# Mean squares of q and k: two float32r products of a split square in place of one float32 product

## The chip, the cores and the metric

The kernel runs on one core of a Trainium2 chip. The metric is device time in microseconds (us). Engines are named as in the profile: PE (matrix products and transposes), PEld (PE's weight loads, a row of its own), DVE (VectorE), ACT (ScalarE), POOL (GpSimd), SP (the queue that starts most transfers).

## What is computed

Two layers of a hybrid backbone work on 1024 latent tokens and 256 context tokens. The part that matters here is the normalisation of queries and keys, ahead of two kinds of attention (A: a window, with rotary positions; B: a neighbourhood on a grid):

```
def rms_norm(x, g):
    x32 = x.astype(jnp.float32)
    y = x32 * lax.rsqrt(jnp.mean(x32 * x32, axis=-1, keepdims=True) + EPS)
    return (y * g.astype(jnp.float32)).astype(x.dtype)
...
    qa = rope_2d(rms_norm(aq.reshape(bsz, t_len, A_HEADS, HEAD_DIM), a_qn))
    ka = rope_2d(rms_norm(ak.reshape(bsz, t_len, A_KV_HEADS, HEAD_DIM), a_kn))
...
    qb = rms_norm(bq.reshape(bsz, t_len, B_HEADS, HEAD_DIM), b_qn)
    kb = rms_norm(bk.reshape(bsz, t_len, B_HEADS, HEAD_DIM), b_kn)
```

The mean runs over the 64 channels of a head.

## The kernel before

Activations lie transposed: channels on the 128 partitions, tokens along the free dimension, in three chunks of 512, 512 and 256 tokens. Nearly all projections and attention products take float32 operands that were split into a float32r high part and a float32r rest; `split` does it with a cast on ACT and a subtraction on DVE, `split_w` for weights with a cast on ACT and a subtraction on POOL. A projection is then three products, high by high, high by rest and rest by high.

A channel block of 128 holds two heads. For each such block of q or k (a "pair"), `qk_norm` is called once for each chunk when the projection's last product is done. It squares the projection on ACT into `sq`, multiplies it with the gain on DVE into `raw`, and puts `finish` on a timer of T["ms"] ns. `finish` multiplies `sq` with a 128x128 matrix `blk` (two 64x64 blocks of 1/64) in one float32 product, which gives every channel the mean square of its head. DVE adds epsilon (`me`, L743), ACT and DVE make the inverse root in the buffer of `sq` (L749 to L754), the rotary of branch A runs on DVE and POOL (L758 to L761), and `to_dram` splits the result on POOL (L771, L772) and sends it to DRAM, from where attention loads it.

A layer has 39 such calls: in branch B four pairs with k and q, in branch A one k block and four q pairs, three chunks each. In all there are 78, of which 52 have 512 columns and 26 have 256.

PE's instructions are in program order. The other engines' order comes from a scheduler. The program order is made while the kernel is built, by the class `Weave`: a clock `W.now` goes forward by an assumed time for every product (`mm`: n / 0.6 ns for float32, n * 17 / 38.4 for float32r), `W.later` puts a piece of work on a timer of that clock, and between timed pieces the clock's owner takes "dense" work, first q, k and v projections (`need`), then gate projections (`spare`, tiles gt and sg). The attention itself is a chain of steps no closer than T["pace"] ns. Products end in PSUM tiles of the tags d, s, t and o; the mean square takes one of the three t tiles, which the transposes of the attention weights (pt) also use.

Tiles have a fixed number of buffers, here `qraw` 2 (also used for the cached keys and values, kc and vc, and for the v projection, vr) and `qsq` 2. Whoever takes a buffer waits for the last user of the tile that had it before.

Of the kernel before, what the change touches and what calls it, by code (L numbers as in the profile page):

```python
# [15 lines left out]
P = 128  # L16
# [9 lines left out]
HD = 64  # L26
# [50 lines left out]
PSB = {"d": 2, "s": 2, "t": 3, "o": 1}  # L77
LGB = ("s", "t")
LDB = ("d", "t")
T = dict(f1=9, f2=2, kc=10000, c0=10000, cq=1, gx=3, nx=8000, yo=1500, yi=1000, aq=9000, ac=7000, ms=2000, v=3200, tok=8600, scale=1100, t0=3400, tb=2200, o=2200, soft=7600, pace=9000, lg=320, lr=8500, cv=16000, le=4200)  # L80


class Weave:
# [107 lines left out]
def trunk(nc, tc, ctx, I, K, O):  # L191
# [46 lines left out]
    nc.scalar.dma_start(cst[:, :384], K["k_const"][:, :384])  # L238
    nc.scalar.dma_start(cst[:, 384:], K["k_const"][:, 768:])
    ident, blk, ones_d, sel = cst[:, 0:128], cst[:, 128:256], cst[:, 256:384], cst[:, 384:386]  # L240
    fill = cp.tile([P, 2], F32, name="fill")
    nc.vector.memset(fill[:, 0:1], EPS)
    nc.vector.memset(fill[:, 1:2], 1e-37)
# [182 lines left out]
    def split(hi, lo, x):  # L426
        nc.scalar.copy(hi, x)  # L427
        nc.vector.tensor_sub(lo, x, f32(hi))  # L428
# [40 lines left out]
    def blocked(t):  # L469
        return t.rearrange("p (r a c) -> p a r c", r=8, a=8)  # L470
# [256 lines left out]
    def attention(l, H, ap):  # L727
# [2 lines left out]


        def qk_norm(ps, N, gain, rope_c0, name, then, blocks=False):
            raw = ap.tile([P, 512], F32, tag="qraw", name=f"{name}_raw", bufs=2)
            sq = ap.tile([P, 512], F32, tag="qsq", name=f"{name}_sq", bufs=2)
            src, to = (blocked(ps), in_blocks) if blocks else (ps, lambda t: t)
            nc.scalar.activation(to(sq[:, :N]), src, AF.Square)
            nc.vector.tensor_scalar(to(raw[:, :N]), src, gain, None, ALU.mult)

            def finish():
                ms = ps_tile("t", f"{name}_ms")  # L740
                mm(ms[:, :N], blk, sq[:, :N], True, True)
                me = cp.tile([P, 512], F32, tag="g2", name=f"{name}_me", bufs=3)
                nc.vector.tensor_scalar(me[:, :N], ms[:, :N], EPS, None, ALU.add)  # L743
                if not loaded:
                    exp_ln(me[:, :N])
                    loaded.append(True)
                rs = sq

                nc.scalar.activation(rs[:, :N], me[:, :N], AF.Ln)  # L749
                nc.scalar.activation(rs[:, :N], rs[:, :N], AF.Exp, scale=-0.5)  # L750
                nc.vector.tensor_tensor(raw[:, :N], raw[:, :N], rs[:, :N], ALU.mult)
                nc.scalar.activation(rs[:, :N], rs[:, :N], AF.Square)
                nc.vector.tensor_tensor(rs[:, :N], me[:, :N], rs[:, :N], ALU.mult)
                nc.vector.scalar_tensor_tensor(raw[:, :N], rs[:, :N], -3.0, raw[:, :N], ALU.add, ALU.mult)  # L754
                if rope_c0 is not None:
                    cs = ap.tile([P, 2, 512], F32, tag="stage", name=f"{name}_cs", bufs=2)
                    dma(cs, K["k_rope"][:, :, rope_c0:rope_c0 + N])
                    nc.vector.stream_shuffle(rs, raw, [(i + 16) % 32 for i in range(32)])  # L758
                    nc.gpsimd.tensor_tensor(rs, rs, cs[:, 1], ALU.mult)
                    nc.gpsimd.tensor_tensor(raw, raw, cs[:, 0], ALU.mult)  # L760
                    nc.gpsimd.tensor_add(raw, raw, rs)  # L761
                then(raw[:, :N])
            W.later(T["ms"], finish)
# [17 lines left out]
        def k_jobs(br, p, cond):  # L781
            name = f"{br}{l}_{p}"
            perm, rope = br == 1, br == 0
            c0w = O_BK + p * P if br else O_AK
            h0 = 2 * p if br else 0
            out = O[4] if br else O[2]

            def start():
                t = ap.tile([P, 4, P], F32, tag="qraw", name=f"kc{name}", bufs=2)
                src = I["cache_kb"] if br else I["cache_ka"]  # L790
                dma(t, src[0, l, :, h0:h0 + 2].rearrange("(j p) h d -> p j (h d)", p=P))

                def cached():
                    pt = ps_tile("t", f"kct{name}")
                    for j in range(4):
                        transpose(pt[:, j * P:(j + 1) * P], t[:, j], ident)
                    to_dram(pt, NPAST, f"kc{name}", k_put(br, p, NTOK, NPAST), True)
                W.later(T["kc"], cached)

            def evac(ci, ps):  # L800
                c0, N = CHUNKS[ci]

                def then(kn):
                    if c0 >= NLAT:
                        def to_tokens():
                            pt = ps_tile("t", f"kt{name}")
                            for j in range(2):
                                transpose(pt[:, j * P:(j + 1) * P], kn[:, j * P:(j + 1) * P], ident)
                            ko = ap.tile([P, 2, P], F32, tag="Y", name=f"ko{name}", bufs=2)
                            nc.scalar.copy(ko, pt[:, :2 * P].rearrange("p (j m) -> p j m", j=2))  # L810
                            dma(out[0, l, :, h0:h0 + 2].rearrange("(j p) h d -> p j (h d)", p=P), ko)
                        W.later(T["tok"], to_tokens)
                    to_dram(kn, N, f"k{name}_{ci}", k_put(br, p, c0, N))
                    W.mark(("K", br, l, p, ci), 4000)
                qk_norm(ps, N, dcol[l][:, 2 * br + 1:2 * br + 2], c0 if rope and c0 < NLAT else None,
                        f"k{name}_{ci}", then, perm and c0 < NLAT)
            W.need.append((cond, job(w_in, c0w, (0, 1, 2), lambda ci: H.cols(ci), evac, f"k{name}", start)))

        def v_jobs(br, p, cond):
# [5 lines left out]

            def evac(ci, ps):
                c0, N = CHUNKS[ci]
                vr = ap.tile([P, 512], F32, tag="qraw", name=f"vr{name}_{ci}", bufs=2)
                lat = perm and c0 < NLAT
                nc.scalar.copy(in_blocks(vr) if lat else vr[:, :N], blocked(ps) if lat else ps)  # L830

# [45 lines left out]
        class Keys:  # L877
# [16 lines left out]

            def load_v(c):
                h0 = 2 * c.p if c.br else 0
                t = ap.tile([P, 4, 2, HD], F32, tag="qraw", name=f"vc{c.name}", bufs=2)
                src = I["cache_vb"] if c.br else I["cache_va"]
                dma(t, src[0, l, :, h0:h0 + 2].rearrange("(j p) h d -> p j h d", p=P))
                c.V = {}  # L900
                for n, b0, nb in (("lat", 0, 8), ("ctx", 8, 2)):
                    c.V[n] = ap.tile([P, nb, 2, 2, HD], F32R, tag=f"V{n}", name=f"V{n}{c.name}")
                    dma(f32(c.V[n]), v_d[l][c.br][c.p][:, b0:b0 + nb])
                c.V["past"] = ap.tile([P, 4, 2, 2, HD], F32R, tag="Vpast", name=f"Vpast{c.name}")
                split(c.V["past"][:, :, :, 0], c.V["past"][:, :, :, 1], t)
                c.at["V"] = W.now + 7000
# [631 lines left out]
```

## Time and profile before

| what | value |
|---|---|
| median of 3 runs | 3151.2 us (3148.72 to 3158.55) |
| the profiled execution's own time | 3155.3 us |
| its span, from first to last instruction | 3153.5 us |
| its mean granted TensorE clock | 0.992 |
| PE busy | 3080.7 us, 98% |
| PEld busy | 2629.2 us, 83% |
| DVE, ACT, POOL busy | 1786.2 us, 1708.8 us, 971.1 us |

The times of one engine add up over instructions. PE's matrix instructions overlap in time, so their durations do not say how often one can start; the distance of their starts does.

### The profile page before, as it was taken

How to read it: one execution, taken by the hardware profiler on the slowest of the kernel's cores; microseconds unless marked ns; L12 is line 12 of the kernel's file. 1: busy time of each engine (PE TensorE's matmuls, PEld its weight loads, DVE VectorE, ACT ScalarE, POOL GpSimd, SP SyncE). 2: the span in 40 equal slices, each digit the busy share in tenths (PEclk: the TensorE clock that was granted, in tenths of full speed). 3: DMA queues.
4: the chain of work that ended last, by engine and by line, in shares of the span. 5: the costliest groups of instructions: out<-in, count | busy, mean ns of one | idle time of the engine just before them, and what ended most of it. 6: DMA issues, size and time to landing. Idle time of an engine off the chain costs nothing.

```text
span 3153.5 us, 48110 instructions
## 1 busy us (share of the span) xinstructions
PE 3080.7 (98%) x17421; PEld 2629.2 (83%) x17421; DVE 1786.2 (57%) x3293; ACT 1708.8 (54%) x3591; POOL 971.1 (31%) x815
## 2 busy tenths in 40 slices
PE   8999999999999999999999999999999999999999
PEld 5777788888888888888888888888888888888887
DVE  5666366666666664355463553665675666655431
ACT  4677355555556564343356873655555556654422
POOL 3454322222222121245343443222231221112632
PEclk8999999999999999999999999999999999999999
DMA  8654555545532332663442226455555332347543
GB/s 277 174 177 136 162 142 152 157 110 160 157 99 81 96 94 79 225 203 115 147 146 70 79 91 183 118 147 147 138 142 154 95 96 80 98 140 241 163 146 101
DMA packets 447434, 435.03 MB, mean 138 GB/s; under 512 B 75120, under 2 KB 368604, under 8 KB 445916
## 3 DMA queue, kind: packets, MB, share of 16 engines
q1 hardware_dynamic: 441212, 414.92, 44.1%
q0 software_dynamic: 5664, 16.83, 1.6%
q8 instruction: 137, 2.24, 0.3%
q14 instruction: 101, 0.83, 0.1%
q10 hardware_dynamic: 320, 0.21, 0.0%
HBM read 298.12 MB, written 137.29 MB: 138 GB/s over the span
## 4 chain that ended last, share of the span: by engine, by line
PE 64%; DVE 6%; POOL 3%; ACT 2%; issue 2%; DMA 2%; SPq 0%; ACTq 0%; POOLq 0%; DVEq 0%
PE gt L218 14%; PE sg L218 10%; PE br L218 6%; PE o L218 5%; PE po L218 5%; PE pt L225 5%; PE q L218 4%; PE sc L218 3%; PE k L218 3%; PE v L218 2%; PE sl L218 2%; PE cx L218 2%; POOL acc L1242 1%; PE lg L218 1%; DVE gl L1241 1%
## 5 line engine op out<-in xcount | busy, mean ns | idle before, releaser
L427 ACT CAST PT<-pt 128x512 fp32r<-128x512 f32 (+2 forms) x528 | 273.3, 536 | 304.2 <-PE pt L225 299.8
L428 DVE TENSOR_TENSOR PT<-pt,PT 128x512 fp32r<-128x512 f32 (+2 forms) x528 | 320.9, 622 | 99.3 <-ACT PT L427 96.6
L981 DVE TENSOR_REDUCE st<-sc 128x1 f32<-128x512 f32 x256 | 176.0, 687 | 269.8 <-PE sc L218 269.3
L218 PE MATMUL gt<-hhl,wgt_h 128*128 128x512 f32 x736 | 299.3, 407 | 1.4 <-ACT wgt_h L422 1.3
L218 PE MATMUL gt<-hhl,wgt_l 128*128 128x512 f32 x736 | 290.2, 394 | 1.1 <-POOL wgt_l L423 1.1
L218 PE MATMUL gt<-hll,wgt_h 128*128 128x512 f32 x736 | 290.0, 394 | 0.0
L225 PE MATMUL pt<-cst,P 128*128 128x128 f32 x1856 | 272.7, 273 | 4.6 <-ACT ko L810 4.1
L423 POOL TENSOR_TENSOR wgt_l<-wgt_r,wgt_h 128x512 fp32r<-128x512 f32 x110 | 174.0, 1590 | 290.2 <-ACT wgt_h L422 280.4
L225 PEld LDWEIGHTS pt<-cst,P 128*128 128x128 f32 x1856 | 217.6, 141 | 9.7 <-ACT ko L810 4.5
L218 PE MATMUL po<-z,wpo_h 128*128 128x512 f32 (+1 forms) x768 | 211.2, 362 | 7.2 <-ACT z L427 4.5
L218 PE MATMUL br<-yl,wbr_h 128*128 128x512 f32 (+1 forms) x576 | 205.2, 356 | 1.6 <-DVE yl L428 1.6
L218 PE MATMUL br<-yh,wbr_h 128*128 128x512 f32 (+1 forms) x576 | 204.7, 355 | 0.3 <-DVE gl L1241 0.3
L218 PE MATMUL br<-yh,wbr_l 128*128 128x512 f32 (+1 forms) x576 | 204.4, 355 | 0.0
L1003 ACT ACTIVATE P<-sc,st 128x512 f32<-128x512 f32 x256 | 175.2, 684 | 53.7 <-DVE st L997 52.8
L423 POOL TENSOR_TENSOR wsg_l<-wsg_r,wsg_h 128x512 fp32r<-128x512 f32 x48 | 66.3, 1387 | 374.7 <-ACT wsg_h L422 353.3
L1005 ACT ACTIVATE P<-sl,st 128x384 f32<-128x384 f32 (+1 forms) x320 | 170.7, 533 | 17.6 <-DVE st L993 17.3
L218 PE MATMUL sc<-Kpast,Q 128*128 128x512 f32 x512 | 168.3, 410 | 9.0 <-ACT P L1003 9.0
L218 PE MATMUL o<-PT,Vpast 128*128 128x256 f32 x1024 | 176.0, 294 | 0.9 <-DVE PT L428 0.3
L218 PEld LDWEIGHTS gt<-hhl,wgt_l 128*128 128x128 f32 x736 | 138.5, 188 | 33.8 <-POOL wgt_l L423 1.5
L218 PEld LDWEIGHTS gt<-hhl,wgt_h 128*128 128x128 f32 x736 | 139.0, 189 | 32.6 <-issue 4.7
L218 PEld LDWEIGHTS po<-z,wpo_h 128*128 128x128 f32 x768 | 136.1, 190 | 31.9 <-ACT z L427 5.8
L218 PEld LDWEIGHTS gt<-hll,wgt_h 128*128 128x128 f32 x736 | 139.2, 189 | 25.8 <-issue 0.5
(350 smaller groups left out, 8535.7 us busy)
## 6 DMA issues: line engine op xcount, KB each, us to landing
Q<-q_d SPq DMA_DIRECT2D x160, 256.0 KB
gl<-g_d SPq DMA_DIRECT2D x48, 640.0 KB
wgt_r<-in_w_in_dram SPq DMA_DIRECT2D x110, 256.0 KB
g_d<-tgt SPq DMA_DIRECT2D x92, 256.0 KB
wa<-in_w_ada_dram POOLq DMA_DIRECT2D x64, 256.0 KB, 4.0
wpo_r<-in_w_out_dram SPq DMA_DIRECT2D x64, 256.0 KB
yg<-y_d SPq DMA_DIRECT2D x24, 640.0 KB
yr<-s_d SPq DMA_DIRECT2D x24, 640.0 KB
```

The costliest lines, as they stand in the source:

```text
L218: nc.tensor.matmul(out, a, b, start=start, stop=stop)
L225: nc.tensor.transpose(out, x, idn)
L423: nc.gpsimd.tensor_sub(lo, r, f32(hi))
L427: nc.scalar.copy(hi, x)
L428: nc.vector.tensor_sub(lo, x, f32(hi))
L981: nc.vector.tensor_reduce(cm, psc, AX.X, ALU.min)
L1003: nc.scalar.activation(pt[:, nl * P:(nl + 4) * P], psc, AF.Exp, bias=m, scale=-1.0, accum_out=sums[:, t, x, 1:2])
L1005: nc.scalar.activation(pt[:, :nl * P], loc, AF.Exp, bias=m, scale=-1.0, accum_out=sums[:, t, x, 0:1])
L1241: nc.vector.scalar_tensor_tensor(g, g, 1.0, ps, ALU.add, ALU.mult)
L1242: (nc.vector if b == 0 and k >= KD - 2 else nc.gpsimd).tensor_add(z, z, g)
```

## The change

The sum over a head's channels is taken from the square's two float32r parts, in two products that add up in one PSUM tile, with a float32r copy of `blk`. The parts have a tile of their own, `qtwo`, which has one buffer (the pool's default). `split` is called right behind the square and the gain, ahead of the timer. `qraw` and `qsq` get three buffers. T["ms"] goes from 2000 to 4500, T["pace"] from 9000 to 8800. The descriptor space of the transfers that POOL starts goes from its default of 16384 to 8192 bytes per partition. The four other lines that changed name qraw's new buffer count.

```
-T = dict(f1=9, f2=2, kc=10000, c0=10000, cq=1, gx=3, nx=8000, yo=1500, yi=1000, aq=9000, ac=7000, ms=2000, v=3200, tok=8600, scale=1100, t0=3400, tb=2200, o=2200, soft=7600, pace=9000, lg=320, lr=8500, cv=16000, le=4200)
+T = dict(f1=9, f2=2, kc=10000, c0=10000, cq=1, gx=3, nx=8000, yo=1500, yi=1000, aq=9000, ac=7000, ms=4500, v=3200, tok=8600, scale=1100, t0=3400, tb=2200, o=2200, soft=7600, pace=8800, lg=320, lr=8500, cv=16000, le=4200)
...
     ident, blk, ones_d, sel = cst[:, 0:128], cst[:, 128:256], cst[:, 256:384], cst[:, 384:386]
+    blk_r = cp.tile([P, P], F32R, name="blk_r")
+    nc.scalar.copy(blk_r, blk)
...
         def qk_norm(ps, N, gain, rope_c0, name, then, blocks=False):
-            raw = ap.tile([P, 512], F32, tag="qraw", name=f"{name}_raw", bufs=2)
-            sq = ap.tile([P, 512], F32, tag="qsq", name=f"{name}_sq", bufs=2)
+            raw = ap.tile([P, 512], F32, tag="qraw", name=f"{name}_raw", bufs=3)
+            sq = ap.tile([P, 512], F32, tag="qsq", name=f"{name}_sq", bufs=3)
             src, to = (blocked(ps), in_blocks) if blocks else (ps, lambda t: t)
+
             nc.scalar.activation(to(sq[:, :N]), src, AF.Square)
             nc.vector.tensor_scalar(to(raw[:, :N]), src, gain, None, ALU.mult)
+            two = ap.tile([P, 2, 512], F32R, tag="qtwo", name=f"{name}_two")
+            split(two[:, 0, :N], two[:, 1, :N], sq[:, :N])

             def finish():
                 ms = ps_tile("t", f"{name}_ms")
-                mm(ms[:, :N], blk, sq[:, :N], True, True)
+                mm(ms[:, :N], blk_r, two[:, 0, :N], True, False)
+                mm(ms[:, :N], blk_r, two[:, 1, :N], False, True)
...
-    nc = bacc.Bacc("TRN2", target_bir_lowering=False, num_devices=1)
+    nc = bacc.Bacc("TRN2", target_bir_lowering=False, num_devices=1, dynamic_dma_scratch_size=8192)
```

How PE's order changes shows at the start of the first layer's attention. The names are those of pair 0: k_0_1 and k_0_2 are its second and third chunk of k, q_0_0 the first chunk of q, k_0_1_ms and k_0_2_ms their mean squares. The projection of k_0_1 ended before these rows. Before:

```order
L218 MATMUL k_0_2_3369<-hhc_5_1040,wk_0_4_l 128x256
L218 MATMUL k_0_1_ms<-k_0_1_sq,cst 128x512
L218 MATMUL k_0_2_3369<-hhc_6_1049,wk_0_4_h 128x256
...
L218 MATMUL k_0_2_3369<-hhc_7_1058,wk_0_4_l 128x256
L218 MATMUL q_0_0_3425<-hhl_0_230,wq_0_0_h 128x512
...
L218 MATMUL q_0_0_3425<-hhl_2_234,wq_0_0_l 128x512
L218 MATMUL k_0_2_ms<-k_0_2_sq,cst 128x256
L218 MATMUL q_0_0_3425<-hhl_3_236,wq_0_0_h 128x512
```

And now:

```order
L218 MATMUL q_0_0_3422<-hll_2_237,wq_0_0_h 128x512
L218 MATMUL q_0_0_3422<-hhl_2_236,wq_0_0_l 128x512
L218 MATMUL k_0_1_ms<-k_0_1_two,blk_r 128x512 x2
L218 MATMUL q_0_0_3422<-hhl_3_238,wq_0_0_h 128x512
...
L218 MATMUL q_0_0_3422<-hhl_5_242,wq_0_4_l 128x512
L218 MATMUL k_0_2_ms<-k_0_2_two,blk_r 128x256 x2
L218 MATMUL q_0_0_3422<-hhl_6_244,wq_0_4_h 128x512
```

Both mean squares have moved back by several projection products, and the third chunk's now stands nine products of 512 columns behind the second's, where before there were fifteen (six of 256 columns and nine of 512).

On ACT the cast of the split stands between the other work. The same place, with what each row waits for in brackets (PE, DVE, Pool, Activation are engines, DMAHW and DMASW transfers). Before:

```order
L736 ACTIVATE k_0_1_sq<-k_0_1_3309 128x512 [waits DMASW4_49,DMASW3_49,DMASW6_49,DMASW2_49,DMASW7_49,DMASW0_49,PE_49]
L752 ACTIVATE k_0_0_sq<-k_0_0_sq 128x512 [waits DVE_49]
L422 CAST wv_0_0_h<-wv_0_r_3413 128x512 [waits DMAHW5_49,PE_49,Pool_49]
L427 CAST kc_0_st<-kct_0_3349 128x512 [waits DMASW6_49,DMASW2_49]
L422 CAST wv_0_4_h<-wv_0_r_3419 128x512 [waits DMAHW6_49,PE_49,Pool_49]
L749 ACTIVATE k_0_1_sq<-k_0_1_me 128x512 [waits DVE_49,Activation_49]
L736 ACTIVATE k_0_2_sq<-k_0_2_3369 128x256 [waits PE_49]
```

And now:

```order
L739 ACTIVATE k_0_1_sq<-k_0_1_3314 128x512 [waits PE_49]
L756 ACTIVATE k_0_0_sq<-k_0_0_sq 128x512 [waits Activation_49]
L429 CAST k_0_1_two<-k_0_1_sq 128x512 [waits Activation_49]
L739 ACTIVATE k_0_2_sq<-k_0_2_3378 128x256 [waits PE_49]
L424 CAST wv_0_0_h<-wv_0_r_3410 128x512 [waits DMAHW5_49,Pool_49]
L758 ACTIVATE k_0_0_sq<-k_0_0_sq 128x512 [waits DVE_49]
L424 CAST wv_0_4_h<-wv_0_r_3416 128x512 [waits DMAHW6_49,Pool_49]
L429 CAST k_0_2_two<-k_0_2_sq 128x256 [waits PE_49,Activation_49]
L429 CAST kc_0_st<-kct_0_3358 128x512 [waits DMASW6_49,DMASW2_49]
L755 ACTIVATE k_0_1_sq<-k_0_1_me 128x512 [waits DVE_49]
```

Two casts have come in. The second, k_0_2_two, waits for PE: its buffer is free only when the products of k_0_1_ms have read it.

## Rows read from the trace of the kernel before

**Rows 1.** The page's part 1: busy time, share of the span, instructions.

```profile
PE 3080.7 (98%) x17421; PEld 2629.2 (83%) x17421; DVE 1786.2 (57%) x3293; ACT 1708.8 (54%) x3591; POOL 971.1 (31%) x815
```

**Rows 2.** Both attention stages: PE, PEld, DVE, ACT, POOL busy; PEclk, DMA, GB/s.

```profile
326.00:1262.00 936.00, 917.85 (x5473) 802.13 (x5473) 567.09 (x1241) 526.86 (x1348) 224.54 (x204) 0.99 0.43 123
1890.00:2810.00 920.00, 905.39 (x5426) 785.94 (x5425) 567.36 (x1239) 522.90 (x1341) 220.35 (x200) 1.00 0.45 124
```

**Rows 3.** What PE waited for: total us, times, longest.

```profile
PE q_ms L218 <- ACT q_sq L736: 6.0, 2, 3.0
...
PE pt L225 <- ACT ko L810: 4.1, 2, 2.1
PE vt L225 <- ACT vr L830: 3.6, 2, 2.1
```

**Rows 4.** Timeline of PE around two mean squares (start, duration, instruction).

```profile
347.87 1.02 PE L218 MATMUL k_ms<-k_sq,cst 128*128 128x512 f32 x2
348.32 0.68 PE L218 MATMUL k<-hhc,wk_h 128*128 128x256 f32 x1
348.84 0.28 PE L218 MATMUL k<-hlc,wk_h 128*128 128x256 f32 x1
348.96 0.28 PE L218 MATMUL k<-hhc,wk_l 128*128 128x256 f32 x1
...
351.50 0.59 PE L218 MATMUL k_ms<-k_sq,cst 128*128 128x256 f32 x2
351.75 0.58 PE L218 MATMUL q<-hhl,wq_h 128*128 128x512 f32 x1
352.16 0.39 PE L218 MATMUL q<-hll,wq_h 128*128 128x512 f32 x1
352.39 0.40 PE L218 MATMUL q<-hhl,wq_l 128*128 128x512 f32 x1
```

**Rows 5.** Groups of the mean squares' tiles: duration ns min/median/max, first and last start, forms.

```profile
L218 PE MATMUL q_ms<-q_sq,cst x96: 377/591/796, 357.4 to 2678.1; 128*128 128x512 f32 x64, 128*128 128x256 f32 x32
...
L218 PEld LDWEIGHTS k_ms<-k_sq,cst x60: 186/189/192, 340.7 to 2333.2; 128*128 128x128 f32 x60
L218 PE MATMUL k_ms<-k_sq,cst x60: 377/592/644, 340.9 to 2333.4; 128*128 128x512 f32 x40, 128*128 128x256 f32 x20
```

**Rows 6.** ACT's cast of a 128x512 tile, by line: busy, mean ns.

```profile
L422 ACT CAST wgt_h<-wgt_r 128x512 fp32r<-128x512 f32 x110 | 66.8, 621 | 40.7 <-DMA wgt_r<-in_w_in_dram 21.5 <-PE q L218 9.2 <-PE gt L218 3.3
```

**Rows 7.** DVE on k's tiles: two SBUF sources (L751), one PSUM source (L743, q).

```profile
L751 DVE TENSOR_TENSOR k_raw<-k_raw,k_sq x30: 396/692/1720, 345.3 to 2338.1; 128x512 f32<-128x512 f32 x20, 128x256 f32<-128x256 f32 x10
...
L743 DVE TENSOR_SCALAR q_me<-q_ms x48: 404/680/693, 358.8 to 2680.4; 128x512 f32<-128x512 f32 x32, 128x256 f32<-128x256 f32 x16
```

**Rows 8.** Timeline of all engines at 902 us, idle time before in brackets.

```profile
901.89 2.98 POOL L423 TENSOR_TENSOR wgt_l<-wgt_r,wgt_h 128x512 fp32r<-128x512 f32 x2
901.95 1.79 DVE L751 TENSOR_TENSOR q_raw<-q_raw,q_sq 128x512 f32<-128x512 f32 x1
903.66 1.23 DVE L1000 TENSOR_TENSOR st<-st,sink 128x1 f32<-128x1 f32 x1
904.92 0.29 ACT L1001 ACTIVATE st<-sink,st 128x1 f32<-128x1 f32 x1 [2.15 <-DVE st L1000]
...
907.29 1.22 PE L218 MATMUL q_ms<-q_sq,cst 128*128 128x256 f32 x2 [3.04 <-ACT q_sq L736]
```

**Rows 9.** Timelines at 780 and 811 us.

```profile
780.54 0.75 DVE L737 TENSOR_SCALAR q_raw<-q,dcol 128x512 f32<-128x512 f32 x1 [1.30 <-POOL k_st L772]
...
783.02 0.44 PE L225 MATMUL pt<-cst,P 128*128 128x128 f32 x2 [2.07 <-ACT ko L810]
...
810.89 0.59 ACT L830 COPY vr<-v 128x512 f32<-128x512 f32 x1 [3.73 <-POOL q_st L772]
```

**Rows 10.** ACT's timeline at the kernel's start.

```profile
7.98 0.22 ACT L331 ACTIVATE sl<-ccol 128x16 f32<-128x16 f32 x1 [4.10 <-DVE ccol L330]
```

**Rows 11.** The page's part 3: the queue of POOL's transfers: packets, MB, share.

```profile
q0 software_dynamic: 5664, 16.83, 1.6%
```

More of the change, by code (lines that the diff above doesn't have):

```diff
@@ L788, in start @@
             def start():
-                t = ap.tile([P, 4, P], F32, tag="qraw", name=f"kc{name}", bufs=2)
+                t = ap.tile([P, 4, P], F32, tag="qraw", name=f"kc{name}", bufs=3)
                 src = I["cache_kb"] if br else I["cache_ka"]
@@ L827, in evac @@
                 c0, N = CHUNKS[ci]
-                vr = ap.tile([P, 512], F32, tag="qraw", name=f"vr{name}_{ci}", bufs=2)
+                vr = ap.tile([P, 512], F32, tag="qraw", name=f"vr{name}_{ci}", bufs=3)
                 lat = perm and c0 < NLAT
@@ L896, in load_v @@
                 h0 = 2 * c.p if c.br else 0
-                t = ap.tile([P, 4, 2, HD], F32, tag="qraw", name=f"vc{c.name}", bufs=2)
+                t = ap.tile([P, 4, 2, HD], F32, tag="qraw", name=f"vc{c.name}", bufs=3)
                 src = I["cache_vb"] if c.br else I["cache_va"]
```

## Prediction

> **What bounds the kernel now.** I read the shares of the engines first, then the stages that hold the change, then PE's own waits, and last single places in the timeline. PE is busy for 98% of the span and DVE and ACT for a little over half of it [rows 1]. All 78 mean squares lie in the two attention stages, from 326 to 1262 us and from 1890 to 2810 us. There PE is busy for 917.85 of 936 us and 905.39 of 920 us, DVE for some 567 us and ACT for some 525 us, at a granted clock of 0.99 to 1.00, the upper of its two levels [rows 2]. PE's instructions are in one order, so what PE no longer does there shortens the span, unless a wait comes up in its place. PE's waits are few: those which touch q, k and v tiles are 6.0, 4.1 and 3.6 us, twice each, once in each layer for q_ms and pt [rows 3].
>
> **What a mean square costs.** A busy time does not say it, since PE's durations overlap; the starts do. The float32 product of 512 columns starts at 347.87, and the second product behind it at 348.84, 0.97 us later. The product between them takes 0.12 us, as the step from 348.84 to 348.96 shows, so the mean square held PE for 0.85 us [rows 4]. That of 256 columns goes from 351.50 to 352.16, 0.66 us, less one 512-column product of 0.23 (352.16 to 352.39): 0.43 us [rows 4]. In each case the trace shows it as two matrix records and two weight loads [rows 5].
>
> A float32r product takes 0.23 us for 512 columns and 0.12 us for 256 [rows 4], so two take 0.46 and 0.24 us. The saving is 0.39 us for each of 52 mean squares, 20.3 us, and 0.19 us for each of 26, 4.9 us. **Together 25.2 us**, half in each attention stage. Its two ends: if a pair of products cost nothing beyond its columns and hid behind its neighbours' ends, there is no more than that to gain; if, as the profile's records suggest, each of the two passes needs its weight load and the load were the limit, the gain is nothing (a rival below).
>
> **What the split adds.** One ACT cast and one DVE subtraction for each of 78, in the attention stages. A cast of 128x512 from SBUF takes 0.621 us [rows 6]; with that for all 78, an upper bound since 26 are half as wide, ACT gets 48 us more, 24 us a stage on 525. The subtraction reads two SBUF tiles, as L751 does, whose median is 0.692 and whose smallest is 0.396 us [rows 7]: 52 x 0.692 + 26 x 0.396 = 46 us, 23 us a stage on 567. Both engines stay below two thirds of a stage, and PE's other products are the cover. If that cover were gone and PE waited through every subtraction, it would cost 46 us, more than the saving.
>
> The subtraction has an upper end of its own. L751 takes up to 1.720 us, while L743, which reads PSUM, never exceeds 0.693 [rows 7]. At 901.95 such an instruction took 1.79 us while two POOL subtractions ran from 901.89 to 904.87; the next, of one column, took 1.23 us; ACT waited 2.15 us for that, and PE 3.04 us at the next mean square [rows 8]. So DVE instructions with two SBUF sources are held up by POOL's. The Trainium skill, in "SBUF — State Buffer", section "SBUF: two separate sides", says that DVE with two SBUF inputs and a GpSimd instruction that reads SBUF share a port pair as an exclusive lock; the trace agrees (1.79 us beside 0.692). By that rule each of the 78 subtractions may be held up, which speaks against the change. I take the median, because more than half of L751's 30 instructions stayed near it in the same surroundings. Were all 78 held for the whole 1.720 us, DVE would have 134 us more, 67 a stage, and stand at 634 of 936 us, still not the bound.
>
> **What the wait times do.** T["ms"] puts the product later by 2.5 us of PE's program. The way to it was one ACT square; now it is a square, a cast and a subtraction, some 2 us by these rows. The order gives PE about 4.6 us of work (18 products of 0.23 us and one pair of 0.46) between the third chunk's last product and its mean square, where there were nine products of 0.23 us, 2.1 us. So the slack grows from about 1.4 to about 2.6 us. Two things are late next. The normalised q and k reach DRAM 2.5 us later, which delays the attention chain only where it waits for them; PE then has projections and gates to do, which in both orders last beyond the chain's last value product. And `qtwo` has one buffer: the next chunk's cast waits until PE has done the chunk before. Fourteen casts carry that wait, as k_0_2_two in the order above; behind it on ACT stand the evacuation of kc and the chain of k_0_1, and later the casts of attention weights that PE needs. In ten places only nine products of 512 columns, 2.07 us, stand between the two mean squares, and in them ACT casts (0.62 us at most [rows 6]) and DVE subtracts (0.40 to 0.69 us [rows 7]). That fits, if neither engine is occupied. Bounds: nothing, or 10 x 3.04 us, the longest wait of this kind [rows 8], 30 us. I take 0.4 us in each of the ten, 4 us, near the lower end, because 2.07 us leaves about 0.8 us of slack.
>
> T["pace"] lets the chain's steps follow each other 0.2 us sooner. It adds no work to PE and moves gate products behind the chain; I cost it at nothing, with the cover named above.
>
> **What the third buffer gives.** `raw` waited for POOL's last use of the tile two chunks earlier: DVE 1.30 us at 780.54, after which PE waited 2.07 us for a t tile; ACT's vr, in the same tag, waited 3.73 us at 810.89 [rows 9], after which PE waited for the transposes of v. Three buffers take away the waits of this kind: between nothing and the 4.1 + 3.6 us of pt and vt, and with the 6.0 us of q_ms, whose product now comes later, 13.7 us [rows 3]. I take 4 us, half of the first two, since the same DVE and POOL remain congested in these places.
>
> **At nothing:** the cast of `blk` (ACT is idle for 4.10 us at the start, before 7.98 us [rows 10]; without that, below 0.6 us once), and the smaller descriptor space. POOL's queue moved 5664 packets in the whole kernel [rows 11], 354 for each of 16 DMA engines. If that space did limit, POOL would wait in the stage before attention; I have no row for it and leave it to the range.
>
> **The sum.** -25.2 + 4 - 4 = -25 us: 3130 us against the profiled execution's 3155.3 us. That execution is 4.1 us above the median, so against the median of 3151.2 us I predict **3126 us**, a span of about 3128 us in a profile like this one. The likeliest case's own range is plus and minus 9 us, 3117 to 3135.
>
> **Rivals.**
> - *More than the products.* All of the 13.7 us of waits go too, and no new ones come: 3151.2 - 25.2 - 13.7 = 3112 us. For it: three buffers and the later product meet their causes. Against: at 902 us the cause was POOL's hold on DVE [rows 8], which stays.
> - *The saving is taken back.* Either weight loads set the pace, or a wait of 0.32 us for each of the 78 uses it up; 3151 us, or half of it, 3139. Weight loads: each takes about 0.189 us [rows 5], and the number stays two. Against it, products of 256 columns start every 0.12 us with a load each, and the mean square held PE for more than twice its two loads [rows 4]. The Trainium skill, in "Perfetto Trace Analysis", section "Identifying the Most-Contended Engine", calls matmul busy time a bad measure and weight-load busy time a good one. By that rule, PE with 83% of loads [rows 1] has room and keeps all of its loads, and the time would be 3151 us; the steps of the starts bear this out little.
> - *Slower: the one buffer of qtwo.* A cast that waits for PE holds ACT, ACT's casts of attention weights come late, and PE waits. Priced at the wait of 3.04 us [rows 8] in each of fourteen places: 42.6 us less the 25.2, 3169 us. It decides from 1.8 us a place; from 2.5 us the kernel is slower by more than 0.3%. Against it: the slack of 0.8 us, and that ACT is idle for over 40% of the stage.
>
> **How the numbers follow.** A measurement of this kernel can tell about 0.3%, 9.5 us, from no change. Chances: my forecast 0.62, more 0.14, taken back 0.16, slower 0.08. Of the third, half ends within 9.5 us of before, and half is still faster. Faster 0.84, same 0.08, slower 0.08. The range leaves out the slower case and the outer part of the first and third: 3108 to 3147.
>
> **What would show it.** The two attention stages shorter by about 12 us each and the other stages within 2 us; mean squares of 0.46 and 0.24 us by their starts; DVE busier by some 46 us and ACT by up to 48; no wait of DVE for POOL at `raw`. New idle time of PE before ms products, named after the cast or subtraction of `two`, would speak for the slower rival; a mean square that still holds PE for 0.85 us, for weight loads. The prediction is wrong if PE's waits in the attention stages change by more than 10 us either way.

## The result and the profile after

The changed kernel takes 3172.8 us in the median (3168.1 to 3175.5) against 3151.2 us: a ratio of 1.0062, 95% interval 1.0046 to 1.0078. It is slower by 0.6%, some 20 us, where 25 us less were predicted. The profiled execution took 3169.9 us, its span is 3168.1 us.

The page's part 1 of the changed kernel [rows 1 has it for before]:

```profile
PE 3067.1 (97%) x17421; PEld 2625.3 (83%) x17421; DVE 1832.1 (58%) x3371; ACT 1745.6 (55%) x3670; POOL 987.8 (31%) x815
```

PE is busy for 13.6 us less. DVE has 45.9 us more to do and ACT 36.8 us more, as forecast. The span is longer all the same, so PE waits more. Windows show where. First those of before, cut from the first k product to the last value product of each layer, then from there to the first product of the merge (columns as in [rows 2]):

```profile
329.00:1251.00 922.00, 906.82 (x5411) 792.62 (x5412) 565.84 (x1238) 523.03 (x1340) 219.12 (x199) 0.99 0.42 122
1251.00:1327.00 76.00, 76.00 (x405) 65.70 (x404) 25.15 (x20) 32.73 (x45) 16.32 (x11) 1.00 0.68 233
1896.00:2809.00 913.00, 898.39 (x5384) 779.72 (x5383) 566.96 (x1238) 521.32 (x1338) 218.71 (x199) 1.00 0.45 123
2809.00:2851.00 42.00, 42.00 (x219) 35.39 (x218) 21.47 (x16) 22.02 (x27) 7.83 (x5) 1.00 0.81 279
```

The same four of the changed kernel:

```profile
326.00:1261.00 935.00, 911.12 (x5509) 802.01 (x5510) 588.42 (x1277) 543.96 (x1386) 229.83 (x203) 0.99 0.42 122
1261.00:1318.00 57.00, 57.00 (x306) 49.44 (x305) 27.38 (x20) 29.75 (x39) 14.31 (x9) 1.00 0.81 280
1888.00:2823.00 935.00, 899.23 (x5387) 784.89 (x5386) 588.73 (x1277) 539.90 (x1377) 225.14 (x199) 0.99 0.44 120
2823.00:2865.00 42.00, 42.00 (x218) 35.40 (x218) 20.76 (x16) 22.13 (x27) 7.03 (x5) 1.00 0.79 280
```

In the first layer attention takes 13 us longer but does gate products that before stood in the gap behind it, which is 19 us shorter: 6 us are gained. In the second layer attention is 22 us longer and nothing comes back. That is the loss. In the two attention windows together PE is idle for 59.7 us, where before it was 29.8. PE's list of waits in the changed kernel:

```profile
PE sc L218 <- ACT P L1009: 22.5, 24, 3.0
PE q_ms L218 <- DVE q_two L430: 10.5, 14, 2.2
PE k_ms L218 <- DVE k_two L430: 8.6, 6, 2.1
...
PE sl L218 <- DMA Klat<-k_d: 6.7, 3, 2.7
...
PE o L218 <- DVE Y L1072: 3.6, 3, 1.9
```

The waits of [rows 3] for ko, vr and sq are gone. New are 19.1 us in 20 places for the subtraction of `two`; the attention chain's scores, which wait for ACT's exponentials P of earlier scores, cost 22.5 us in 24 places (9.0 in 13 before), and scores that wait for k's transfers (Klat) 6.7 us (0.6 before).

The products themselves came out as predicted. PE's timeline has the pair of 512 columns from 348.24 to 348.69, 0.45 us, where the float32 product took 0.85 [rows 4]:

```profile
348.00 0.40 PE L218 MATMUL q<-hhl,wq_l 128*128 128x512 f32 x1
348.24 0.62 PE L218 MATMUL k_ms<-k_two,blk_r 128*128 128x512 f32 x2
348.69 0.40 PE L218 MATMUL q<-hhl,wq_h 128*128 128x512 f32 x1
...
350.77 0.28 PE L218 MATMUL k_ms<-k_two,blk_r 128*128 128x256 f32 x1
351.66 0.38 PE L218 MATMUL k_ms<-k_two,blk_r 128*128 128x256 f32 x1 [0.61 <-DVE k_two L430]
```

The last line shows the price: the second product of the pair waits for the rest of the squares. One of the long waits, with what DVE has ahead of it (timeline at 1006 us):

```profile
1005.65 0.63 ACT L429 CAST q_two<-q_sq 128x512 fp32r<-128x512 f32 x1
...
1005.83 1.28 POOL L425 TENSOR_TENSOR wsg_l<-wsg_r,wsg_h 128x512 fp32r<-128x512 f32 x1 [21.19 <-ACT wsg_h L424]
...
1006.07 1.60 DVE L760 SCALAR_TENSOR_TENSOR q_raw<-q_sq,q_raw 128x512 f32<-128x512 f32 x1
...
1007.93 0.72 DVE L764 STREAM_SHUFFLE q_sq<-q_raw 128x512 f32<-128x512 f32 x1
...
1008.03 0.39 PE L218 MATMUL q_ms<-q_two,blk_r 128*128 128x512 f32 x1
...
1008.60 1.01 DVE L430 TENSOR_TENSOR PT<-pt,PT 128x512 fp32r<-128x512 f32 x2
...
1008.72 1.27 POOL L765 TENSOR_TENSOR q_sq<-q_sq,q_cs 128x512 f32<-128x512 f32 x1 [1.61 <-DVE st L1006]
...
1009.53 1.01 DVE L430 TENSOR_TENSOR q_two<-q_sq,q_two 128x512 fp32r<-128x512 f32 x1
...
1010.60 0.50 PE L218 MATMUL q_ms<-q_two,blk_r 128*128 128x512 f32 x1 [2.18 <-DVE q_two L430]
```

The cast is done at 1006.28, the subtraction starts at 1009.53, 3.25 us later: DVE first finishes the chunk before (L760, L764) and the chain's two subtractions for PT. It then takes 1.01 us beside POOL's instruction, where its median is 0.684. L760, which also reads two SBUF tiles, took 1.60 us beside POOL's weight split of 1005.83, where its median is 0.692. That is the hold of [rows 8], and the place is no exception: at 18 of the 20 places DVE lost 0.7 to 1.2 us in this way, in instructions with two SBUF sources that lasted longer than the median of their form while POOL ran, from the cast on to the end of the subtraction and with no idle time of DVE behind them. Taken off each wait, and never more than the wait, it is 12.5 of the 19.1 us. This is an estimate from the durations of this one trace; no run takes POOL's work away.

The other place is the end of attention in the second layer. PE's timeline there:

```profile
2780.92 0.28 PE L218 MATMUL sg<-hhc,wsg_l 128*128 128x256 f32 x1
2781.04 0.63 PE L218 MATMUL sc<-Kpast,Q 128*128 128x512 f32 x2
2781.50 0.51 PE L218 MATMUL sl<-Klat,Q 128*128 128x384 f32 x2
2781.85 0.60 PE L225 MATMUL pt<-cst,P 128*128 128x128 f32 x4
2785.41 1.22 PE L218 MATMUL sc<-Kpast,Q 128*128 128x512 f32 x2 [2.97 <-ACT P L1009]
```

The last gate product is done at 2781; the chain goes on alone until its last value product at 2823, 42 us later. Before, these two were 6 us apart (2803.0 and 2809.2). Windows of that end show what it does to PE's clock:

```profile
2763.00:2781.00 18.00, 18.00 (x113) 16.06 (x112) 8.89 (x23) 8.42 (x24) 0.00 (x0) 1.00 0.27 81
2781.00:2786.00 5.00, 2.03 (x11) 1.58 (x10) 2.49 (x5) 3.65 (x11) 2.50 (x2) 0.85 0.29 85
2786.00:2791.00 5.00, 3.01 (x11) 2.50 (x10) 2.70 (x7) 2.32 (x7) 0.00 (x0) 0.50 0.16 46
2791.00:2796.00 5.00, 3.41 (x13) 2.72 (x13) 3.22 (x9) 2.44 (x7) 0.00 (x0) 0.63 0.08 26
2796.00:2824.00 28.00, 21.36 (x119) 17.67 (x119) 14.02 (x32) 11.95 (x33) 0.00 (x0) 0.88 0.02 6
```

PE is busy for 47.8 of these 61 us; in the last 61 us of before it was 59.4. After the gap at 2782 the granted clock goes to 0.50, the lower level of 1.2 GHz, and the same two score products take 1.22 us instead of 0.63.

### The profile page after: what moved, and what is told of

Its sections match the earlier page's. It is cut to its first block, busy times and chain, and to the rows that moved or that the text cites. A ratio compares the mean times of both kernels' runs of the same rounds, so it can differ in the third digit from the quotient of the medians.

```text
span 3168.1 us, 48251 instructions
## 1 busy us (share of the span) xinstructions
PE 3067.1 (97%) x17421; PEld 2625.3 (83%) x17421; DVE 1832.1 (58%) x3371; ACT 1745.6 (55%) x3670; POOL 987.8 (31%) x815
## 4 chain that ended last, share of the span: by engine, by line
PE 73%; DVE 11%; ACT 7%; DMA 4%; issue 3%; POOL 2%; SPq 1%; ACTq 0%; POOLq 0%; DVEq 0%
PE gt L218 15%; PE sg L218 10%; PE o L218 6%; PE pt L225 6%; PE br L218 6%; PE po L218 5%; PE q L218 5%; PE k L218 4%; PE v L218 4%; PE sc L218 3%; PE sl L218 3%; PE cx L218 2%; POOL acc L1248 1%; PE lg L218 1%; DMA Klat<-k_d 1%
## 5 line engine op out<-in xcount | busy, mean ns | idle before, releaser
L218 PE MATMUL sc<-Kpast,Q 128*128 128x512 f32 x512 | 166.8, 407 | 22.6 <-ACT P L1009 22.5
L218 PEld LDWEIGHTS gt<-hll,wgt_h 128*128 128x128 f32 x736 | 139.6, 190 | 25.9 <-issue 0.5
```

Of the source, the lines that this page charges most:

```text
L218: nc.tensor.matmul(out, a, b, start=start, stop=stop)
```

## The experiments

All were run in five rounds beside the kernel before; the ratio is to it. Differences in us between two of them are differences of ratios times 3151.

**The times alone, and the split with the old ms.** e1 is the kernel before with the two new numbers, e2 the changed kernel with ms back.

```diff
 e1: -ms=2000, pace=9000
     +ms=4500, pace=8800
 e2: -ms=4500
     +ms=2000
```

> The kernel before with only the two numbers of the table changed (ms 4500, pace 8800): no split, two buffers. Theory A (the later mean squares delay the attention chain in the planned clock, the gate products are used up early, and the end of the second layer's attention has nothing beside the chain): the last gate product before the second layer's last value product ends some 35 to 42 us ahead of it, where before it was 6 us, PE has gaps there, and the time is 3151 + 20 = about 3170 us, less up to 6 us for the waits of q_ms that the later place takes away: 3164 to 3172. Theory B (the single buffer of the split makes PE wait): nothing of the kind can come without the split, so 3145 to 3153 us.

> The changed kernel with ms back at 2000 (pace 8800 stays). By the order PE then has 4.7 us of work behind the last gate product of the second layer's attention, where the changed kernel has 18.0. Theory A: the tail is covered again, some 24 us come back, 3172.8 - 24 = 3149 us, a few more if PE then waits for the split at more mean squares: 3145 to 3157. Theory B: the product comes 2.5 us earlier behind a longer way of ACT and DVE, so the waits at ms grow from 19 us to 30 us or more and the time is 3172 to 3190 us.

e1: 3207.8 us, 1.0179 (1.0166 to 1.0192). e2: 3198.4 us, 1.0148 (1.0134 to 1.0163). Both lie outside every range that was given. By the tail I mean the time from the end of the last gate product to the end of the last value product in the second layer's attention. In e1 the tail opened as A says (39.9 us), but transposes of v waited 15.1 us for ACT's vr and scores 26.4 us for P as well: the later product holds `raw` and `sq` longer, and with two buffers that is paid at once (e9 below, with three, has no such wait of v). In e2 the tail was closed (9.2 us) and PE waited 61.5 us for `two`, in 65 places. So both theories hold a part: the split needs the later product, and the later product opens the tail.

**A second buffer; earlier marks.**

```diff
 e3: -two = ap.tile([P, 2, 512], F32R, tag="qtwo", name=f"{name}_two")
     +two = ap.tile([P, 2, 512], F32R, tag="qtwo", name=f"{name}_two", bufs=2)
     -dynamic_dma_scratch_size=8192
     +dynamic_dma_scratch_size=4096
 e4: e3, and
     -W.mark(("K", br, l, p, ci), 4000)
     +W.mark(("K", br, l, p, ci), 1500)
     -W.mark(("Q", br, l, p, ci), 4000)
     +W.mark(("Q", br, l, p, ci), 1500)
```

> The changed kernel with a second buffer for the split tile (and 4096 instead of 8192 bytes for descriptors, which makes the room). Theory B: the waits of PE at ms products for the split (19.1 us) shrink to a few us, and with them the ACT casts of attention weights that stood behind them: 3172.8 - 20 = about 3153 us or less. Theory A: the tail of the second layer's attention stays as it is, since the order of PE is the same, and what is gained is at most the half of those waits that lies ahead of the tail: 3163 to 3173 us. If the smaller descriptor space costs something, POOL's DMA issues take longer and the time may rise.

> The same with two buffers, and ms still at 4500, but the two marks from which the planner takes q and k as landed brought forward by 2500 ns (4000 to 1500), so that the planned clock sees the chain start when it did before. By the order PE has 4.7 us of work behind the last gate product. Theory A: the tail is covered, the saving of the products (25 us) shows: 3172.8 - 24 - (0 to 15) = 3134 to 3149 us. Theory B: only the second buffer counts, so the same time as with the two buffers alone. If the chain in truth waits for q and k, PE waits at the first scores of groups instead, and some of it is given back.

e3: 3168.3 us, 1.0059 (1.0045 to 1.0073), not to be told from the changed kernel; PE's waits for `two` are still 16.7 us. The single buffer is not the cause, and half the descriptor space costs nothing that shows. e4: 3163.6 us, 1.0044 (1.0031 to 1.0056). The tail closed (9.2 us), and from the second layer's first score product to its last value product it now takes 863 us, where the changed kernel takes 879. But the planner now took k and q as landed too early: PE waited 12.5 us for Klat's transfers (6.7 in the changed kernel), and the second layer's attention began 18 us later (1906.7 for 1888.6 us). In the first layer these waits are 5.1 us longer; the rest of the 18 us is open. Nothing of the saving came out.

**Cover for the tail; the subtraction ahead on DVE; no subtraction.** e7 leaves the rest of the squares out and adds the rounded part twice, so its mean is not the right one (it is twice too large); it tells the time of the same products without the subtraction.

```diff
 e5: -gx=3
     +gx=1
 e6: -split(two[:, 0, :N], two[:, 1, :N], sq[:, :N])
     +with tc.high_priority(400): split(two[:, 0, :N], two[:, 1, :N], sq[:, :N])
 e7: -split(two[:, 0, :N], two[:, 1, :N], sq[:, :N])
     +nc.scalar.copy(two[:, 0, :N], sq[:, :N])
     -mm(ms[:, :N], blk_r, two[:, 1, :N], False, True)
     +mm(ms[:, :N], blk_r, two[:, 0, :N], False, True)
 e8: e5 and e6
```

> The changed kernel with gx 1 instead of 3: two gate jobs of the second layer (the same PE work in sum) are done in that layer's attention instead of before it. The marks, ms and the split stay. By the order no PE work but the chain's last product then stands behind the last gate product, where 18.0 us stand in the changed kernel. Theory A (the uncovered tail costs): the waits in the last 60 us of that attention (17 us above nominal) and the dip of the granted clock to 0.5 in 2786 to 2791 us go away, 3172.8 - 18 to 21 = 3152 to 3155 us. If the gates are missed where they were taken away, less. Theory B (waits for the split alone): no change, 3170 to 3176 us.

> The changed kernel with a higher priority for the cast and the subtraction of the split, nothing else: the order of PE's instructions is the same to the row, the subtractions stand further forward on DVE. Theory B (PE waits since the subtraction stands behind DVE's other work, not because of the one buffer): the 19.1 us of waits at ms products shrink to some 6 us, and the time to about 3172.8 - 13 = 3160 us, less what work moved behind the subtraction gives back (PT's subtraction for the chain above all): 3158 to 3168. Theory A: no change by itself in the tail, so never below 3155 us.

> The changed kernel without the subtractions: the second product takes the rounded squares again, so the rest of the squares is left out of the mean, and PE has the same products. DVE has 78 instructions less. Theory B: PE's waits for the split (19.1 us) go down to those for the cast alone, below 3 us, and the time to about 3156 us, with DVE some 46 us less busy; that would be the whole price of the subtraction. Theory A: the tail stays, since the order of PE is about the same, so not below 3152 us.

> Both mends together: gx 1 and the split at a higher priority. If the tail and the waits for the split are the two causes and independent, their gains add up: 3172.8 - 20 - 13 = 3140 us, which is below the kernel before. If one hides the other (a PE that stops waiting at ms reaches the chain's waits sooner), 3145 to 3155 us.

e5: 3162.1 us, 1.0035 (1.0022 to 1.0048). The tail is covered (0.5 us, PE busy for 61.0 of the last 61 us), but only 8.5 of some 20 us came back. The gate jobs had covered a wait in the stage that they were taken from, as PE's timeline of e5 there shows:

```profile
1627.58 0.79 PE L218 MATMUL gt<-hhl,wgt_h 128*128 128x512 f32 x1 [8.76 <-ACT hhl L568]
...
1632.79 0.49 PE L218 MATMUL gt<-hll,wgt_h 128*128 128x512 f32 x1
1633.12 0.39 PE L218 MATMUL gt<-hhl,wgt_l 128*128 128x512 f32 x1
```

After 8.76 us without work PE's 512-column products take 0.79 us at first and 0.39 again from 1633.12 on; the granted clock is 0.52 from 1627.5 to 1633 us and 0.83 in the mean of 1609 to 1639 us.

e6: 3160.0 us, 1.0029 (1.0017 to 1.0041), 10.4 us better with PE's order unchanged. Its waits for `two` fall from 19.1 to 2.2 us:

```profile
PE k_ms L218 <- DVE k_two L430: 1.2, 2, 0.6
PE q_ms L218 <- DVE q_two L430: 1.0, 4, 0.4
```

Scores wait somewhat more for P (25.9 us), values for Y (5.4). e8: 3152.4 us, 1.0003 (0.9994 to 1.0012): the two mends add up (8.5 + 10.4 against 18.6) and bring the kernel back to the time of before, no further. e7: 3141.2 us, 0.9968 (0.9958 to 0.9978): the subtraction is worth 29.6 us, nearly three times what its place in the queue (e6) explains, and this with the tail still open (43 us). Theory A's floor of 3152 was wrong.

**The parts of the change one at a time.** e9 has the float32 product back in place of the split, with all else of the change; e10 is the kernel before with the third buffers and the smaller descriptor space only.

```diff
 e9:  -split(two[:, 0, :N], two[:, 1, :N], sq[:, :N])
      -mm(ms[:, :N], blk_r, two[:, 0, :N], True, False)
      -mm(ms[:, :N], blk_r, two[:, 1, :N], False, True)
      +mm(ms[:, :N], blk, sq[:, :N], True, True)
 e10: -tag="qraw", name=f"{name}_raw", bufs=2    (and each other qraw, qsq)
      +tag="qraw", name=f"{name}_raw", bufs=3
 e11: e6, and gx=2
 e12: e6, and ms=2600
```

> The changed kernel with the float32 product of the squares back in place of the split and its two products: ms 4500, pace 8800 and the third buffers stay, so that it is the run of the new times on the kernel before plus the third buffers. Theory C (the split saves 28 us of products and costs the 31.6 us that leaving the subtraction out gave back; the later ms costs the rest): 3172.8 + 28 - 32 = 3169 us. Theory D (the split is a gain as it is, since DVE has room, and only the new times cost): 3172.8 + 25 = 3198 us. If the third buffers do not pay for the later ms, 3205 us, as with two buffers.

> The kernel before with three buffers in place of two for raw and squares (and 8192 bytes for descriptors), nothing else. As the prediction priced it, the freed waits of pt and vt give 4 us: 3148 us; at most 13.7 us with q_ms: 3138 us. If they only move to the next wait, 3152 us.

> The split at a higher priority and gx 2: one gate job more in the second layer's attention instead of two. With gx 1 PE had nothing to do for 9 us in the stage that the gate jobs were taken from, and the tail had more than it needs. By the order 8.9 us of PE work stand behind the last gate product (18.0 with gx 3, 0.1 with gx 1). If the tail is worth its waits, the time is 3160 - 13 + 3 = 3145 to 3152 us; if the 9 us in the stage before come with the first gate job already, 3155 us.

> The split at a higher priority with ms 2600 and gx 3 as in the changed kernel. By the order 4.7 us stand behind the last gate product. Theory A: the tail is covered without moving gates, 3160 - 18 = 3142 us. Theory B: the mean square comes 1.9 us earlier, and PE waits for the split again, between 10 us and the 61 us of the run with ms 2000 without the priority: 3152 to 3190 us. The sum of both, with 15 us of waits: 3157 us.

e9: 3163.1 us, 1.0038 (1.0024 to 1.0052); e10: 3149.8 us, 0.9992 (0.9983 to 1.0001). So the third buffers give 2.5 us (between 5 and nothing), and the smaller descriptor space that comes with them costs nothing that shows. The tail of e10 is 6.2 us, that of e9 39.4 us; the new times on top of the buffers cost 14.5 us with no split in the kernel; with two buffers they cost 56 us (e1). From e9 to the changed kernel the split, products and all, adds 7.6 us: theory C. e11: 3154.4 us, 1.0011 (1.0002 to 1.0019): one gate job covers half of the tail (16.7 us left) and is no better than two. e12: 3151.5 us, 1.0004 (0.9995 to 1.0013): the tail closed (9.6 us), waits for `two` of 7.7 us, but a new one that neither theory had:

```profile
PE o L218 <- DVE Y L1072: 17.4, 9, 3.6
```

Value products wait until DVE has taken the last group's result out of the one PSUM bank.

**How the subtraction costs, and the products alone.** e13 and e15 add the rounded part twice, as e7 does, and are for the time alone.

```diff
 e13: -mm(ms[:, :N], blk_r, two[:, 1, :N], False, True)
      +mm(ms[:, :N], blk_r, two[:, 0, :N], False, True)
 e14: e12, and
      -nc.vector.tensor_scalar(to(raw[:, :N]), src, gain, None, ALU.mult)
      +nc.scalar.activation(to(raw[:, :N]), src, AF.Identity, scale=gain)
 e15: (on the kernel before; blk_r and descriptor space as in the change)
      -nc.scalar.activation(to(sq[:, :N]), src, AF.Square)
      +sr = ap.tile([P, 512], F32R, tag="qsr", name=f"{name}_sr", bufs=2)
      +nc.scalar.activation(to(sr[:, :N]), src, AF.Square)
      -mm(ms[:, :N], blk, sq[:, :N], True, True)
      +mm(ms[:, :N], blk_r, sr[:, :N], True, False)
      +mm(ms[:, :N], blk_r, sr[:, :N], False, True)
 e16: (e10, and as e15 with one product)
      +mm(ms[:, :N], blk_r, sr[:, :N], True, True)
```

> The changed kernel in which DVE still does all 78 subtractions, but the second product reads the rounded squares again and not the rest, which is left out of the mean. PE waits for the cast alone. Between the changed kernel (3172.8 us) and the run without the subtractions (3141.2 us) this splits the 31.6 us: if they come from PE's wait for the result, and from what that wait delays, 3141 to 3150 us; if they come from DVE's time (78 x 0.6 us in the queue ahead of the chain's work), 3160 to 3173 us.

> The split at a higher priority, ms 2600, and the scaling of raw by the gain (78 instructions that read PSUM) moved from DVE to ACT; the result is the whole sum. If DVE's time is what costs, the 17.4 us in which PE waits at value products for DVE's Y, and the 6.7 us at the split, go down to some 8, and the time from 3151.5 to 3130 to 3140 us, below the kernel before. If ACT becomes late in its place (its squares, casts and exponentials stand behind 48 us more), PE waits for P and the split instead and the time is 3150 to 3165 us.

> The kernel before in which ACT writes the squares rounded to float32r, and two float32r products read them (the rest is left out of the mean, and the same part is added twice): the cheaper products alone, without a cast, a subtraction, a third buffer or new times. If the products' saving reaches the end, 3151 - 28 = 3123 us. If what PE saves uncovers the chain (by the order 6.6 us behind the last gate product instead of 3.1), 3127 to 3135 us. If PE was never the bound there, 3151 us.

> The kernel before with the third buffers, squares rounded to float32r by ACT and one float32r product of them; the rest of the squares is left out. The products save 52 x 0.63 + 26 x 0.31 = 41 us: 3150 - 41 = 3109 us, if all of it reaches the end. By the order 13.6 us stand behind the last gate product of the second layer, so the tail opens as in the changed kernel, with some 12 us: about 3121 us.

e13: 3155.3 us, 1.0011 (1.0002 to 1.0020), about the middle: 16 us of the subtraction come from PE's wait for its result, 14 us from DVE's time even when nobody waits for the result. In its list scores wait for P for 30.3 us, the most of all runs. Against e7, which lacks only the subtractions, that is 4.3 us more, and the waits for k's transfers are 6.8 us for 0.9: 10.2 of the 14 us stand in these two. e14: 3147.9 us, 0.9995 (0.9986 to 1.0004): DVE is relieved of 45.6 us, but values still wait 15.6 us for Y and means 13.0 us for `two` (7.9 on DVE, 5.1 on ACT). The gain over e12 lies within the intervals, and the forecast of 3130 to 3140 was missed.

e15: 3125.3 us, 0.9916 (0.9902 to 0.9931). The products alone give 26.5 us (31 to 22); the 25.2 us that their starts promised lie within. The two attention windows of e15:

```profile
327.00:1233.00 906.00, 892.31 (x5427) 786.49 (x5427) 562.91 (x1238) 521.49 (x1340) 220.01 (x200) 1.00 0.43 125
...
1877.00:2778.00 901.00, 887.10 (x5381) 777.47 (x5381) 563.23 (x1238) 520.85 (x1338) 218.95 (x199) 1.00 0.45 124
```

They are 16 and 12 us shorter than in the kernel before. e16: 3110.9 us, 0.9874 (0.9859 to 0.9889), the fastest of all: 39.7 us, of which the third buffers have some 2.5 and its products the other 37, where 41 were expected. Its tail is open too, 26.7 us, but PE is still busy for 54.7 of the last 62 us: it is not the tail's length that costs, but PE's idle time in it. It leaves the rest of the squares out; whoever wants it decides whether a mean of rounded squares will do.

**The pace, and POOL.**

```diff
 e17: -pace=8800
      +pace=9000
 e18: -split(two[:, 0, :N], two[:, 1, :N], sq[:, :N])
      +nc.scalar.copy(two[:, 0, :N], sq[:, :N])
      +nc.gpsimd.tensor_sub(two[:, 1, :N], sq[:, :N], f32(two[:, 0, :N]))
```

> The changed kernel with pace back at 9000, ms stays at 4500. By the order 19.3 us of PE work stand behind the last gate product of the second layer (18.0 with 8800), so the tail is the same. If pace costs nothing, as predicted, 3170 to 3176 us. If the chain's closer steps are what crowds DVE, it is faster by 5 us or more, 3160 to 3167.

> The changed kernel with the 78 subtractions on POOL in place of DVE; the result is the whole sum. If the price is DVE's time and DVE's place in the queue, POOL (31% busy) takes it over for nothing: 3172.8 - 14 to 30 = 3143 to 3159 us. If POOL's subtraction of 1.28 us comes later than DVE's and holds DVE's instructions with two SBUF sources up, as the rows at 902 us of the kernel before show, PE's waits at ms grow beyond 19 us: 3175 to 3200 us.

e17: 3156.3 us, 1.0015 (1.0006 to 1.0024), 14.8 us better, although its tail stays open (46.7 us, clock 0.83 in the last 61 us). PE's waits for `two` are halved:

```profile
PE q_ms L218 <- DVE q_two L430: 5.1, 4, 2.2
...
PE k_ms L218 <- DVE k_two L430: 4.4, 4, 1.6
```

So pace was not free. That the 0.2 us between the chain's steps changed which of DVE's chain work stands ahead of the subtractions is my reading of the lists; no run shows it by itself. e18: 3193.7 us, 1.0139 (1.0125 to 1.0153). POOL's subtraction takes 1.286 us in the median, and PE waits 40.8 us for it. The price goes along to POOL and grows. DVE pays as well, as part 1 of the pages of e7 and e18 shows, in this order:

```profile
PE 3057.6 (97%) x17421; PEld 2622.3 (83%) x17421; DVE 1783.9 (57%) x3293; ACT 1746.5 (56%) x3670; POOL 974.1 (31%) x815
PE 3077.0 (96%) x17421; PEld 2632.1 (82%) x17421; DVE 1805.7 (57%) x3293; ACT 1748.1 (55%) x3670; POOL 1067.3 (33%) x893
```

DVE does the same 3293 instructions in both, and is busy for 21.8 us longer where POOL does 78 more.

## Why the prediction was wrong, step by step

The time went the other way, into a case that I had given a chance of 0.08, and the sign of being wrong that the prediction names came: PE's idle time in the attention windows grew by 29.9 us. Two terms failed, the wait for the split, which I had far too small, and the new times, which I had at nothing.

- **Products, -25.2 us: right.** e15 measured -26.5 (-31 to -22). The rival of weight loads is out: their number stayed (17421), their busy share went from 83 to 84%, and the time fell.
- **Third buffers, -4 us: right in kind.** In e10 the wait for vr went and that for ko fell from 4.1 to 1.3 us; the gain is 2.5 us, between 5 and nothing. It has the smaller descriptor space as well, which I had left to the range; it did no harm that shows. What I did not see is that they carry the later product: without them the new times cost 56 us, with them 14.5.
- **Waits for the split, +4 us: the sum's mis-sized term.** I priced ten tight places at 0.4 us "near the lower end, because 2.07 us leaves about 0.8 us of slack". That counted the split's own two instructions against an idle DVE. At 1006 us DVE was busy for 3.25 us between the cast and the subtraction. PE waited 19.1 us in 20 places, and the subtraction as a whole cost 29.6 us (e7): 16 as PE's wait, 14 as DVE's time that the attention chain lacked (e13). That this is my upper bound of 30 is luck: the bound was ten waits of 3.04 us, and no wait was longer than 2.2. I had also named POOL's hold on DVE and set it aside, because it is small against DVE's sum and the median is seldom left. By the durations it has some 12.5 of the 19.1 us. That DVE stands at 58% of the span did not help, since the chain needs it at given moments. The sentence that "PE's other products are the cover" treats a mean busy share as room; that is where the working went wrong.
- **The later ms at nothing: the step that failed.** I wrote that PE "has projections and gates to do, which in both orders last beyond the chain's last value product". In the second layer only gate products that belong to the merge do; the last one in attention ended 42 us ahead of the chain's end. I had not looked for the last gate product in the order of the changed kernel. It is ms that opens the tail: with 4500, and marks and gates as they are, it is open at both paces (42 us, and 46.7 in e17), with 2000 or 2600 it is closed at pace 8800 (9.2 in e2, 9.6 in e12). With no split in the kernel, ms and pace together cost 14.5 us (e9 less e10). How much of that is the tail alone, and how much pace, is not settled: e5, which covers the tail, pays for the cover elsewhere, and no run without the split has only one of the two numbers.
- **Pace at nothing: failed too.** 14.8 us in the changed kernel (e17), by the waits for `two`, which it shares with the third point; the two prices can't be added.
- **The slower rival gave 3169 us**, near the result, but by another mechanism, so that is luck: a second buffer changes nothing that shows (e3). What I had against it, ACT's idle 40%, was beside the point, for DVE was the engine that was late.

The parts close: -26.5 for the products, -2.5 for the buffers, +14.5 for the times, +29.6 for the subtraction make +15 us, against +19.5 measured. The other 4 or so lie in the products: beside the later times and with the cast they give 22.1 us (e9 against e7) and not 26.5. Each part is known to some 3 to 6 us. Only the subtraction's way through the chain's own waits is told by the lists of waits and not by a run of its own.

The Trainium skill, in "SBUF — State Buffer", section "SBUF: two separate sides", has DVE with two SBUF inputs and a GpSimd instruction that reads SBUF exclude each other on a port pair. The rows agree: beside POOL L760 took 1.60 us and the subtraction 1.01 us, for medians of 0.692 and 0.684. I had weighed the rule on DVE's sum; it acted on the moment at which PE needed the result.

## What to carry to other kernels

- An instruction that is added on an engine with a low mean share is priced at the places where somebody waits for its result: list what stands ahead of it in that engine's order there, not its duration and not the share.
- Where PE hides a chain with filler work, ask for the last filler product ahead of the chain's end, before and after; to save PE's work or to delay the chain uses the cover up, and to move filler there uncovers the place that it came from (e5).
- Try the part that saves by itself: squares that ACT writes rounded need no cast, subtraction or new times. One product of them gave some 40 us with the third buffers (e16), where the whole change lost 20; it leaves the rest of the squares out.

## What the runs showed of the hardware

After PE had waited for 2.97 us, up to 2785.41 us of the changed kernel, the granted clock, 1.00 until 2781, was 0.50 from 2786 to 2791 us, and the chain's products took twice as long, 1.22 us for 0.63. The same is seen behind PE's wait of 3.04 us in the kernel before (0.50 from 907.3 to 912 us) and behind the 8.76 us of e5 (0.52 from 1627.5 to 1633 us). Behind the wait of 2.18 us that ended at 1010.60 it stayed at 1.00. An uncovered tail can thus be longer than the sum of its waits, which I had not reckoned with.

POOL slows DVE down where DVE reads two SBUF tiles: single instructions of 0.69 us take up to 1.81 us beside POOL, and 78 more instructions on POOL made DVE's unchanged work 21.8 us longer (e18 against e7).
